# Products of pooled blocks in the middle of a projection unit instead of between two units

## Chip, cores and metric

The kernel runs on one core of a Trainium2 chip. The metric is the device time of one execution in microseconds, the median of several runs. A core has five engines with a queue of instructions each, which they work off in order: PE (TensorE, matrix products into PSUM), DVE (VectorE), ACT (ScalarE), POOL (GpSimd) and SP (SyncE, here only the issue of DMAs). They meet through semaphores: an instruction whose input is not there waits at the head of its queue, and what stands behind it waits too.

## What is computed

One layer of a hybrid encoder over 512 tokens of width 1024, all in float32. The part that matters here is the first sub-layer. The normalised input `h` is multiplied with one wide matrix `w_in`; its columns feed three mixers (a recurrence, a pooling mixer, a sparse attention) and three gates:

```python
h = rms_norm(x, g_mix_pre[l])
(lru_x, lru_gate, pool_in, q, k, v, q_idx, k_idx, w_idx,
 gate_logits) = split_columns(h @ w_in[l], IN_SIZES)
...
yb = multiscale_pool(pool_in, w_pool[l], pool_scale[l])
```

The pooling mixer takes trailing-window means over 2, 4, 8 and 16 tokens in four groups of 128 channels, subtracts the token itself, and multiplies each group with a 128x128 matrix:

```python
def multiscale_pool(p, w_pool, pool_scale):
    ...
    for g, w in enumerate(POOL_WINDOWS):
        start = jnp.maximum(t + 1 - w, 0)
        win_sum = cs[:, 1:, g] - cs[:, start, g]
        count = (t + 1 - start).astype(jnp.float32)[None, :, None]
        means.append(win_sum / count)
    pooled = jnp.stack(means, axis=2) - pf
    mixed = jnp.einsum('bsgc,gcd->bsgd', pooled, w_pool.astype(jnp.float32)).reshape(bsz, s, POOL_WIDTH)
    return (mixed * pool_scale.astype(jnp.float32)).astype(p.dtype)
```

After the mixers follow their merge, an output projection, cross-attention into 256 memory tokens and a SwiGLU feed-forward part.

## The kernel before

**Precision by halves.** Every float32 operand of a product is split into a rounded half (a cast on ACT) and the remainder (a subtraction on DVE or POOL). `mm3` (L89 to L92) issues three matmuls for one product: high by high, high by low, low by high. `halves` (L414 to L416) makes such a pair from a tile: L415 the cast on ACT, L416 the subtraction on DVE.

**Units.** The input stays on the chip, features on partitions, as the pair `hh`, `hl` (8 blocks of 128 features by 512 tokens). A *unit* is the projection of 128 columns of `w_in`: `unit_piece` (L406) runs `mm3` over the 8 feature blocks k = 0 to 7, so 24 matmuls of 128x512, into one PSUM tile. `unit` (L410) is a whole unit and then `give_w`, which gives the weight buffers free.

**Weights.** `take_w` hands out the next unit's weights and lets `prefetch` split ahead: a cast on ACT (L191) and a subtraction on DVE (L195) or in two halves on POOL (L198, L199). There are four buffers for each half, so a new split waits until an earlier unit has read its weights; its raw buffer is then loaded anew by a DMA on SP (L173).

**The stage of the change.** In this order there are four units for the recurrence, four for the pooling groups (`GROUPS` is 2, 0, 3, 1), and four for the queries of the attention. Work that belongs to a unit but needs its result later is kept in three queues of closures, `gates`, `pools` and `products`, and `settle(q, depth)` runs the oldest of a queue until only `depth` are left.

A pooled block goes through three steps. `pool_block(g, ps)` copies the unit's result out of PSUM on ACT (L628) and makes the window sums on POOL by doubling (L632, L633: one, two, three or four additions for windows of 2, 4, 8 or 16). Its `finish` divides and subtracts on DVE (L638, L640) and makes the halves `h`, `l` (L415 on ACT, L416 on DVE). The `product` it returns is one `mm3` on PE with the group's 128x128 matrix (three matmuls that read `h`, `l`, `h` in this order), then scales the result into `yb` (L648 on ACT, L649 on DVE). The products wait one turn each: the product of block 2 is issued in the turn of group 3, that of 0 in the turn of group 1, that of 3 with the first query unit, that of 1 with the second. The third and fourth query unit have none; nor have the first two pooling units.

In the same stretch DVE works off rounds of a top-k search for the attention (L495, L496), which `pump` takes from a background list a few at a time.

**What sets the order.** The program is written as one sequence, but a planner orders the queue of each engine when the kernel is compiled: it goes by the order in which things are written, moved forward or back by `tc.high_priority(offset=...)`, and by when it thinks their inputs are ready. Block work carries an offset that moves it forward (30 for `pool_block`, 100 for `finish`), the weight splits one that moves them back.

Of the kernel before, what the change touches and what calls it, by code (L numbers as in the profile page):

```python
# [17 lines left out]
S = 512  # L18
KD = D // P
# [46 lines left out]
def hybrid_block_kernel(ctx: ExitStack, tc: tile.TileContext, a: dict, out: bass.AP):  # L66
# [22 lines left out]
    def mm3(o, lh, ll, rh, rl, start, stop):  # L89
        T.matmul(o, lh, rh, start=start, stop=False, skip_group_check=True)  # L90
        T.matmul(o, lh, rl, start=False, stop=False, skip_group_check=True)  # L91
        T.matmul(o, ll, rh, start=False, stop=stop, skip_group_check=True)  # L92
# [6 lines left out]
    def pump(ns):  # L99
        while bg and ns > 0:  # L100
            cost, fn = bg.popleft()
            fn()
            ns -= cost
# [75 lines left out]
    def low_on(engines):  # L179
        low[:] = engines  # L180
# [32 lines left out]
    def take_w(ahead=None):  # L213
        while state["split"] <= state["taken"]:
            split_next()
        w = ready.popleft()
        state["taken"] += 1
        prefetch(ahead)
        return w

    def give_w(*ws):
        for w in ws:
            w[2]()
# [45 lines left out]
    ps = PS.take([P, 8])  # L269
# [4 lines left out]
    for q in range(2):  # L274
        ps = PS.take([P, 4, P])
# [130 lines left out]
    def unit_piece(o, w, c0, c1, ks=range(KD)):  # L406
        for k in ks:
            mm3(o[:, c0:c1], w[0][:, k], w[1][:, k], hh[:, k, c0:c1], hl[:, k, c0:c1], k == 0, k == KD - 1)

    def unit(o, w):  # L410
        unit_piece(o, w, 0, S)
        give_w(w)
# [18 lines left out]
    def stacked_queries(src, dst, m):  # L431

        h, l = T2.take([P, S], F32R), T2.take([P, S], F32R)
        halves(src, h, l)
        SP.dma_start(f32(dst[0][0:64, m]), f32(h[0:64]))
        SP.dma_start(f32(dst[0][64:128, m]), f32(l[0:64]))
        SP.dma_start(f32(dst[1][64:128, m]), f32(h[64:128]))
        SP.dma_start(f32(dst[1][0:64, m]), f32(l[64:128]))
        T2.give(h, l)
# [68 lines left out]
    for m in range(1, 4):  # L508
        w = take_w()
        ps = PS.take([P, S])  # L510
# [15 lines left out]
    w = take_w()  # L526
    ps = PS.take([P, S])
# [69 lines left out]
    def lru_roots():  # L597
        for m in range(4):
            sq.append(T2.take([P, S]))
            A.activation(sq[m], tP[:, m], AF.Sqrt)  # L600
# [24 lines left out]
    def pool_block(g, ps):  # L625
        w = 2 << g
        x_, s0, s1 = T2.take([P, S]), T2.take([P, S]), T2.take([P, S])
        A.copy(x_, ps)  # L628
        PS.give(ps)
        src, dst, other, d = x_, s0, s1, 1  # L630
        while d < w:
            G.tensor_add(dst[:, d:], src[:, d:], src[:, :S - d])  # L632
            G.tensor_copy(dst[:, :d], src[:, :d])  # L633
            src, dst, other, d = dst, other, dst, 2 * d

        def finish():
            with tc.high_priority(offset=100):
                V.scalar_tensor_tensor(src[:, :w - 1], src[:, :w - 1], float(w), inv[:, :w - 1],  # L638
                                       op0=OP.mult, op1=OP.mult)
                V.scalar_tensor_tensor(x_, src, 1.0 / w, x_, op0=OP.mult, op1=OP.subtract)  # L640
                h, l = T2.take([P, S], F32R), T2.take([P, S], F32R)
                halves(x_, h, l)
            T2.give(x_, s0, s1)

            def product():
                pz = PS.take([P, S])
                mm3(pz, wpl[:, 0, g], wpl[:, 1, g], h, l, True, True)
                A.activation(yb[0][:, g], pz, AF.Copy, scale=pscale(g))  # L648
                V.scalar_tensor_tensor(yb[1][:, g], pz, pscale(g), f32(yb[0][:, g]),  # L649
                                       op0=OP.mult, op1=OP.subtract)  # L650
                PS.give(pz)
                T2.give(h, l)
            return product
        return finish
# [7 lines left out]
    gates, pools, products = (collections.deque() for _ in range(3))  # L662

    def settle(q, depth, out=None):
        while len(q) > depth:
            r = q.popleft()()
            if out is not None:
                out.append(r)

    low_on("g")  # L670
    for m in range(4):
        w = take_w()
        ps = PS.take([P, S])
# [2 lines left out]
        gates.append(lru_block(m, ps))  # L676
        pump(800)
    low_on("v")
    for g in GROUPS:
        w = take_w()  # L680
        ps = PS.take([P, S])
        unit(ps, w)
        settle(gates, 1 if g == GROUPS[0] else 0)
        settle(products, 0)
        with tc.high_priority(offset=30):
            pools.append(pool_block(g, ps))
        settle(pools, 1, products)
        pump(1000)
    low_on("vg")
    Q = [K8.take([P, 4, S], F32R) for _ in range(2)]  # L690
    for m in range(4):
        w = take_w()
        ps = PS.take([P, S])
        unit(ps, w)
        settle(products, 0)
        stacked_queries(ps, Q, m)
        settle(pools, 0, products)
        PS.give(ps)
        if m == 1:
            lru_roots()  # L700
        pump(2300)
# [132 lines left out]
    for m in range(4):  # L834
        w = take_w()
        ps = PS.take([P, S])
# [159 lines left out]
    for m in range(4):  # L996
        w = take_w()
        ps = PS.take([P, NM])
# [19 lines left out]
    for i in range(4):  # L1018
        w = take_w()
# [67 lines left out]
    for h in range(4):  # L1087
        w = take_w()
        ps = PS.take([P, S])
# [335 lines left out]
```

## Time and profile before

| what | us |
|---|---|
| median of three runs (lowest, highest) | 884.73 (883.75, 884.84) |
| the profiled execution: its time | 883.94 |
| the profiled execution: span of the trace | 882.0 |
| PE busy in the span | 863.5 |
| DVE busy | 608.9 |
| ACT busy | 399.2 |
| POOL busy | 202.1 |
| the eight units of pooling and queries, with their products | 84.28 to about 136 on the span's clock |

In a row of the timeline stand the start on the span's clock, the duration, the engine, the line of the kernel, the operation and what it writes and reads; brackets give the engine's idle time ahead of it and what ended that. In the table by windows stand the stretch, its length, and for PE, weight loads, DVE, ACT and POOL the busy time with the number of instructions, then PE's granted clock, the share of the DMA engines and their rate. In a list of waits stand who waited, for whom, the sum, the times and the longest. `ps` is any PSUM tile, `hh` and `hl` the input, `wh` and `wl` weights of a unit, `t` any of ten work tiles of 128x512 (here mostly those of a block), `k` any of the larger tiles (here the pooling matrices and `yb`).

### The profile page before, as it was taken

The page shows a single profiled execution, that of the slowest core. Times are in us where ns is not written, and L with a number is a line of the kernel's source. Part 1 is how long each engine was busy: PE and PEld are TensorE (multiplying, and loading weights), DVE is VectorE, ACT ScalarE, POOL GpSimd, SP SyncE. Part 2 cuts the span into 40 slices and gives each one's busy share as a digit, 9 for nine tenths or more (in the row PEclk, how much of TensorE's full clock was granted, in tenths as well). Part 3 has the DMA queues.
Part 4 walks back from the last instruction along what each step waited for, and adds up shares of the span by engine and source line. Part 5 has one row for each costly group of instructions (what it writes and reads, how often), then busy time and mean ns, then how long its engine had stood idle before and what let it go on. Part 6 is the DMA issues. An engine that isn't in the chain of part 4 may idle for free.

```text
span 882.0 us, 12995 instructions
## 1 busy us (share of the span) xinstructions
PE 863.5 (98%) x4932; PEld 749.8 (85%) x4932; DVE 608.9 (69%) x1092; ACT 399.2 (45%) x669; POOL 202.1 (23%) x195
## 2 busy tenths in 40 slices
PE   7999999999999999999999999899999999999997
PEld 7888778888888888888888879899999999888885
DVE  7679989964864746342796788887888787732225
ACT  5455443323654445231565554545454555522121
POOL 2322455554434423210110010211111110000000
PEclk9999999999999999999999999999999999999999
DMA  8952237242332237333255301877677765333102
GB/s 246 251 128 76 79 96 192 71 119 80 89 96 72 60 108 260 99 96 95 91 186 154 96 1 36 168 167 174 150 155 157 174 161 143 120 96 96 48 1 97
DMA packets 128443, 105.52 MB, mean 120 GB/s; under 512 B 6200, under 2 KB 112252, under 8 KB 128380
## 3 DMA queue, kind: packets, MB, share of 16 engines
q1 hardware_dynamic: 120028, 89.99, 35.8%
q0 software_dynamic: 5760, 10.49, 7.6%
q10 hardware_dynamic: 2592, 4.20, 1.4%
q8 instruction: 39, 0.64, 0.3%
q14 instruction: 24, 0.20, 0.1%
HBM read 86.31 MB, written 2.10 MB: 100 GB/s over the span
## 4 chain that ended last, share of the span: by engine, by line
PE 81%; DVE 12%; POOL 2%; issue 2%; ACT 1%; DMA 1%; ACTq 0%; DVEq 0%; POOLq 0%
PE ps L91 25%; PE ps L92 25%; PE ps L90 25%; PE ps L473 2%; DVE k L938 1%; PE ps L800 1%; DVE k L954 1%; POOL t L632 1%; DVE hl L325 1%; DVE t L577 1%; DVE work L496 1%; DVE wl L195 1%; DVE m L495 1%; DVE k L963 1%; POOL y L296 1%
## 5 line engine op out<-in xcount | busy, mean ns | idle before, releaser
L191 ACT CAST wh<-raw 128x1024 fp32r<-128x1024 f32 (+1 forms) x104 | 108.5, 1045 | 226.8 <-PE ps L92 103.5
L90 PE MATMUL ps<-hh,wh 128*128 128x512 f32 (+2 forms) x584 | 207.1, 355 | 0.0
L91 PE MATMUL ps<-hl,wh 128*128 128x512 f32 (+2 forms) x584 | 206.2, 353 | 1.0 <-DVE hl L325 1.0
L92 PE MATMUL ps<-hh,wl 128*128 128x512 f32 (+2 forms) x584 | 206.4, 353 | 0.0
L195 DVE TENSOR_TENSOR wl<-raw,wh 128x1024 fp32r<-128x1024 f32 x60 | 74.5, 1246 | 102.8 <-ACT wh L191 102.8
L91 PEld LDWEIGHTS ps<-hl,wh 128*128 128x128 f32 (+1 forms) x584 | 109.1, 187 | 17.0 <-DVE hl L325 1.4
L90 PEld LDWEIGHTS ps<-hh,wh 128*128 128x128 f32 (+1 forms) x584 | 109.2, 187 | 15.9 <-ACT hh L324 0.2
L92 PEld LDWEIGHTS ps<-hh,wl 128*128 128x128 f32 (+1 forms) x584 | 109.0, 187 | 16.0
L90 PE MATMUL ps<-k,wh 128*128 128x256 f32 (+1 forms) x368 | 114.5, 311 | 0.0
L92 PE MATMUL ps<-k,wl 128*128 128x256 f32 (+1 forms) x368 | 113.8, 310 | 0.0
L91 PE MATMUL ps<-k,wh 128*128 128x256 f32 (+1 forms) x336 | 105.1, 313 | 0.0
L198 POOL TENSOR_TENSOR wl<-raw,wh 128x512 fp32r<-128x512 f32 (+1 forms) x44 | 59.3, 1348 | 148.4 <-ACT wh L191 134.2
L296 POOL TENSOR_TENSOR y<-u,half 128x1 f32<-128x1 f32 x26 | 16.0, 619 | 301.5 <-DVE u L293 260.7
L92 PE MATMUL ps<-wh,k 128*128 128x512 f32 x192 | 75.8, 395 | 0.0
L92 PEld LDWEIGHTS ps<-k,wl 128*128 128x128 f32 x368 | 69.2, 188 | 4.4
L90 PEld LDWEIGHTS ps<-k,wh 128*128 128x128 f32 x368 | 69.3, 188 | 4.2
L1215 DVE TENSOR_TENSOR wl<-raw,wh 128x1024 fp32r<-128x1024 f32 x40 | 48.9, 1225 | 31.7 <-ACT wh L1212 29.7
L91 PE MATMUL ps<-wl,k 128*128 128x512 f32 x176 | 69.4, 394 | 0.4 <-DVE wl L195 0.4
L1212 ACT CAST wh<-raw 128x1024 fp32r<-128x1024 f32 x40 | 42.0, 1049 | 61.2 <-PE ps L91 54.9
L90 PE MATMUL ps<-wh,k 128*128 128x512 f32 x176 | 69.0, 394 | 0.0
L91 PEld LDWEIGHTS ps<-k,wh 128*128 128x128 f32 x336 | 63.2, 188 | 4.2
L199 POOL TENSOR_TENSOR wl<-raw,wh 128x512 fp32r<-128x512 f32 (+1 forms) x44 | 61.3, 1393 | 0.0
(256 smaller groups left out, 1691.0 us busy)
## 6 DMA issues: line engine op xcount, KB each, us to landing
raw<-in_w_in SPq DMA_DIRECT2D x45, 512.0 KB, 4.3
raw<-in_w_ffn_in SPq DMA_DIRECT2D x44, 512.0 KB, 4.6
raw<-in_w_ffn_out SPq DMA_DIRECT2D x22, 512.0 KB, 3.6
raw<-in_w_branch SPq DMA_DIRECT2D x12, 512.0 KB, 3.5
raw<-raw POOLq DMA_DIRECT2D x20, 256.0 KB, 3.8
raw<-k POOLq DMA_DIRECT2D x20, 256.0 KB, 3.3
k<-t SPq DMA_DIRECT2D x32, 128.0 KB, 3.0
raw<-in_w_out SPq DMA_DIRECT2D x8, 512.0 KB, 3.5
```

Of the source, the lines that this page charges most:

```text
L90: T.matmul(o, lh, rh, start=start, stop=False, skip_group_check=True)
L91: T.matmul(o, lh, rl, start=False, stop=False, skip_group_check=True)
L92: T.matmul(o, ll, rh, start=False, stop=stop, skip_group_check=True)
L191: copy = A.copy(h, src)
L195: V.tensor_sub(l, src, f32(h))
L198: G.tensor_sub(l[:, :c], src[:, :c], f32(h[:, :c]))
L199: G.tensor_sub(l[:, c:], src[:, c:], f32(h[:, c:]))
L296: G.tensor_tensor(y, u, half, op=OP.pow)
L325: queued(V.tensor_sub(hl[:, 4 * q:4 * q + 4, dst], ps, f32(h)))
L473: T.matmul(ps[:, :n], q[j][:, hp, r], k[i][:, :n], start=i == 0, stop=i == 1, skip_group_check=True)
L1212: copy = A.copy(h, src)
L1215: V.tensor_sub(l, src, f32(h))
```

## The change

A new function `unit_around` takes the place of `unit` in the four pooling units and the four query units. It issues the first half of the unit (k = 0 to 3, 12 matmuls), then whatever waits in `products`, then the second half, and then gives the weights free. The `settle(products, 0)` behind the unit goes. So a product that was written behind the 24th matmul of its unit is now written behind the 12th; the unit's own end is written behind the product. In the pooling loop the products now also come ahead of `settle(gates, ...)`, though no turn has both.

```diff
     low_on("v")
+    def unit_around(ps, w):
+
+        unit_piece(ps, w, 0, S, range(4))
+        settle(products, 0)
+        unit_piece(ps, w, 0, S, range(4, KD))
+        give_w(w)
+
     for g in GROUPS:
         w = take_w()
         ps = PS.take([P, S])
-        unit(ps, w)
+        unit_around(ps, w)
         settle(gates, 1 if g == GROUPS[0] else 0)
-        settle(products, 0)
         with tc.high_priority(offset=30):
             pools.append(pool_block(g, ps))
         settle(pools, 1, products)
...
     for m in range(4):
         w = take_w()
         ps = PS.take([P, S])
-        unit(ps, w)
-        settle(products, 0)
+        unit_around(ps, w)
         stacked_queries(ps, Q, m)
         settle(pools, 0, products)
         PS.give(ps)
```

## The prediction

> **What bounds the kernel now.** I read the page first: span, engine totals, granted clock.
>
> ```profile
> span 882.0 us, 12995 instructions
> PE 863.5 (98%) x4932; PEld 749.8 (85%) x4932; DVE 608.9 (69%) x1092; ACT 399.2 (45%) x669; POOL 202.1 (23%) x195
> PEclk9999999999999999999999999999999999999999
> ```
>
> PE is busy for 863.5 of 882.0 us at full clock. So a change of order can win only what PE waits for, and costs only what new waits it makes PE suffer. Next I cut the stage of the change into units and products (table by windows; first number after the stretch is its length, then PE busy).
>
> ```profile
> 103.75:105.19 1.44, 0.96 (x4) 0.49 (x3) 1.44 (x4) 0.00 (x0) 0.00 (x0) 1.00 0.48 110
> 105.19:110.69 5.50, 5.50 (x25) 4.51 (x24) 5.50 (x12) 2.65 (x4) 3.21 (x4) 1.00 0.23 68
> 110.69:111.39 0.70, 0.70 (x5) 0.56 (x3) 0.70 (x3) 0.00 (x0) 0.62 (x2) 1.00 0.00 0
> 111.39:116.98 5.59, 5.59 (x26) 4.51 (x24) 4.45 (x14) 2.09 (x4) 2.50 (x5) 1.00 0.36 94
> 123.27:125.25 1.98, 1.24 (x5) 0.67 (x4) 1.98 (x6) 1.98 (x4) 0.00 (x0) 1.00 0.00 0
> ```
>
> I name the units that have a product beside them by their columns: U3 (pooled group 3, ends 103.75), U1 (ends 110.69), Q0 (first query unit, ends 116.98), Q1 (ends 123.27). Behind them come the products p2, p0, p3, p1 of the pooled blocks 2, 0, 3, 1, three matmuls each. A unit is 24 matmuls in 5.59 us, 0.233 us each, so half a unit is 2.79 us. A product whose inputs are there takes 0.70 us (p0). p2 takes 1.44 and p1 1.98: PE loses 0.74 + 1.28 = 2.02 us here. That is all there is to win.
>
> What does a product wait for? Its first and third matmul read h (the rounded half of the pooled block, ACT, L415), its second reads l (the remainder, DVE, L416). PE, then DVE, on the timeline:
>
> ```profile
> 98.25 0.40 PE L90 MATMUL ps<-hh,wh 128*128 128x512 f32 x1
> ...
> 101.02 0.39 PE L90 MATMUL ps<-hh,wh 128*128 128x512 f32 x1
> ...
> 103.75 0.40 PE L90 MATMUL ps<-t,k 128*128 128x512 f32 x1
> 104.63 0.50 PE L91 MATMUL ps<-t,k 128*128 128x512 f32 x1 [0.48 <-DVE t L416]
> ...
> 105.19 0.40 PE L90 MATMUL ps<-hh,wh 128*128 128x512 f32 x1
> ...
> 124.68 0.50 PE L91 MATMUL ps<-t,k 128*128 128x512 f32 x1 [0.56 <-DVE t L416]
> ```
> ```profile
> 103.90 0.67 DVE L416 TENSOR_TENSOR t<-t,t 128x512 fp32r<-128x512 f32 x1
> ...
> 106.04 0.68 DVE L416 TENSOR_TENSOR t<-t,t 128x512 fp32r<-128x512 f32 x1
> ...
> 113.56 0.17 DVE L638 SCALAR_TENSOR_TENSOR t<-t,inv 128x15 f32<-128x15 f32 x1 [1.14 <-POOL t L633]
> ...
> 115.64 0.68 DVE L416 TENSOR_TENSOR t<-t,t 128x512 fp32r<-128x512 f32 x1
> ...
> 121.48 0.16 DVE L638 SCALAR_TENSOR_TENSOR t<-t,inv 128x3 f32<-128x3 f32 x1 [2.05 <-POOL t L633]
> ...
> 123.95 0.68 DVE L416 TENSOR_TENSOR t<-t,t 128x512 fp32r<-128x512 f32 x1
> ```
>
> The four L416 end at 104.57, 106.72, 116.32 and 124.63. U3 starts at 98.25 and is at its middle at 101.02 (its 13th matmul); U1, Q0 and Q1 reach theirs at 107.98, 114.18 and 120.48 (starts 105.19, 111.39, 117.68 plus 2.79). So in the middle of its unit only p0 has its l. p2's comes 3.5 us later, p3's 2.1, p1's 4.1.
>
> What sets those times is a chain beside PE. ACT and POOL in this stage:
>
> ```profile
> 98.30 0.70 ACT L586 ACTIVATE t<-ps,ph 128x512 f32<-128x512 f32 x1
> 101.08 0.62 ACT L415 CAST t<-t 128x512 fp32r<-128x512 f32 x1 [2.08 <-DVE t L640]
> 101.60 0.68 ACT L587 ACTIVATE t<-ps,ph 128x512 f32<-128x512 f32 x1
> ...
> 105.27 0.62 ACT L415 CAST t<-t 128x512 fp32r<-128x512 f32 x1 [2.28 <-DVE t L640]
> 105.79 1.04 ACT L191 CAST wh<-raw 128x1024 fp32r<-128x1024 f32 x1
> 106.74 0.58 ACT L628 COPY t<-ps 128x512 f32<-128x512 f32 x1
> ...
> 114.89 0.62 ACT L415 CAST t<-t 128x512 fp32r<-128x512 f32 x1 [6.98 <-DVE t L640]
> 115.41 1.04 ACT L191 CAST wh<-raw 128x1024 fp32r<-128x1024 f32 x1
> 116.36 0.58 ACT L628 COPY t<-ps 128x512 f32<-128x512 f32 x1
> ...
> 122.95 0.62 ACT L415 CAST t<-t 128x512 fp32r<-128x512 f32 x1 [5.42 <-DVE t L640]
> 123.48 1.04 ACT L191 CAST wh<-raw 128x1024 fp32r<-128x1024 f32 x1
> 124.42 0.68 ACT L648 ACTIVATE k<-ps,pc 128x512 fp32r<-128x512 f32 x1
> ```
> ```profile
> 107.40 1.04 POOL L632 TENSOR_TENSOR t<-t 128x511 f32<-128x511 f32 x1 [7.37 <-ACT t L628]
> ```
>
> L628 copies a finished unit out of PSUM, POOL makes the window sums, DVE (L638, L640) the mean, ACT h, DVE l. Block 3's copy at 106.74 starts POOL; DVE waits 1.14 us for its sums; ACT stands 6.98 us before h of block 3; only then come the weight cast (L191) and block 1's copy, at 116.36, though U1 was over at 110.69. Thus block 1's chain starts where block 3's ends, and l of p1 at 124.63 is the end of one chain that begins at 106.74.
>
> **The change part by part.** Nothing is added or taken away: the same 24 + 3 matmuls per unit, the same tile slots in the same order, no DMA moved. Only a product's place goes from behind its unit to behind the unit's 12th matmul; its drain (L648 on ACT, L649 on DVE) may go earlier with it, and the unit's end, with what waits for it, comes 0.70 us or more later.
>
> Does PE's queue really take the product in the middle? The queues are ordered at compile time by a planner that passes over what it thinks not ready, as this late stretch shows, where one unit matmul slips in before the last of eight L800:
>
> ```profile
> 319.33 1.94 PE L800 MATMUL ps<-k,vv 128*128 128x512 f32 x7
> 321.12 0.39 PE L90 MATMUL ps<-hh,wh 128*128 128x512 f32 x1
> 321.35 0.40 PE L800 MATMUL ps<-k,vv 128*128 128x512 f32 x1
> ```
>
> So the question is when the planner thought h and l ready, and the ACT queue tells. h of block 1 (122.95) and a weight cast stand ahead of p3's drain L648 (124.42), which can go as soon as p3 is done, 0.70 us behind Q0 (117.68). A planner that prefers ready work would not have put them first unless it held h of block 1 ready by then, some 5 us earlier than it came; p1's middle of Q1 is 2.8 us after that. Likewise h of block 3 stands ahead of the copy of U1, that is, it was planned by about 110.7 and came at 115.51. And h of block 2 (101.08) stands between the two tanh (L586, L587) of a gate whose matmuls end where U3 starts, at 98.25: planned done by about 99.6, with l some 1.3 us behind (one DVE operation and L416), so by about 101, which is U3's middle. All three products therefore go to the middle, or within a few matmuls of it, and PE then waits there in earnest, since a matmul behind a waiting one in the queue does not pass it.
>
> The sum, on the clock of this execution. p2: l at 104.57, second half of U3 from 105.19 as p2's follower now, so U3 ends at 105.19 + 2.79 = 107.98 instead of 103.75. The weight cast ahead of block 3's copy takes the buffers of U3's own weights, so it moves from 105.79 to about 108.0, and the copy, 0.95 behind, to 108.95: 2.2 us later than 106.74, and with it the whole chain: l of p3 at 118.5, l of p1 at 126.8. PE meanwhile: U1 with p0 inside (no wait) from 107.98 to 114.27; Q0 reaches its middle at 117.06, waits for p3's l until 118.5, goes on at 119.1, ends at 121.9; Q1 reaches its middle at 124.7, waits until 126.8, goes on at 127.45 and ends at 130.24. Now the next unit starts at 125.25. That is **+5.0 us**.
>
> The unknown is how far the chain moves. Put shortly, PE leaves Q1 at l of p1 + 0.62 + 2.79 instead of l of p1 + 0.62: +2.8 us if the chain does not move at all, +5.0 if it moves by 2.2. If the copy is put ahead of the weight cast it moves by about 1.3 (108.0 against 106.74), and the sum is +4.1. I take the middle of the last two, +4.5: the cast stands ahead of the copy in both of the quoted places, but some reordering of ACT and DVE is sure. A reordering that puts L649 in front of block work on DVE would make that work wait for L648; I estimate that at 1 us (the 0.70 of an activation of this size, L586, and some queueing), so the upper end is +6.
>
> Does anything later give it back? From 126 to 420 us PE has one wait, and is busy throughout:
>
> ```profile
> 126.00:205.00 79.00, 79.00 (x344) 64.20 (x343) 65.79 (x113) 26.94 (x33) 44.81 (x33) 1.00 0.48 127
> ```
> ```profile
> PE ps L800 <- DVE k L416: 0.2, 1, 0.2
> ```
>
> So at most 0.2 us there; the later waits hang on PE's own results and move along. The new waits are covered by nothing, since a unit's second half stands behind the product.
>
> Longer waits could also lower the clock. The longest wait that I can check is 2.5 us late in the kernel, after which the clock is full:
>
> ```profile
> PE ps L90 <- ACT t L1274: 2.5, 1, 2.5
> ```
> ```profile
> 560.00:562.00 2.00, 1.90 (x16) 1.90 (x17) 2.00 (x3) 1.62 (x3) 0.00 (x0) 1.00 0.99 248
> ```
>
> My longest wait without a matmul is 2.9 us (h of p2 lets its first matmul go at 101.74; the second goes at 104.63). [...]
>
> **The rivals.** *The place does not move in the queue* (17%): the planner holds l ready only near the unit's end, so the products stay about where they are: within 1 us of 884.7. For it: all four stand right behind their unit now, and nothing in the PE rows shows a product earlier than that. Against it: the order they were written in forbade it until now, and the ACT queue above speaks for an early plan.
>
> *The waits are filled* (8%, the faster side): if the planner sees l late, it has 12 matmuls of the same unit to put ahead of each product's second matmul, where now it stalls. It decides from the point where the planned l is no earlier than the real one, 104.57 for p2 and 124.63 for p1. It gains both stalls, 2.02 us: 882.7. Against it: the planner is early by about 5 us for blocks 1 and 3.
>
> *The clock falls at p2* (4%): a wait somewhat longer than mine, and 12 matmuls at half speed cost 2.8 us more: about 892.
>
> **How the numbers follow.** The forecast has 71%: 883.94 (this execution's time, 1.94 around its span) + 4.5 = 888.4; the median of the three runs is 884.73, 0.79 above, so I set 884.73 + 4.5 = 889.2. The forecast's own range is +2.8 to +6: 887.5 to 890.7. To hold 8 in 10 the range takes in part of the first rival: 884.5 to 890.8. About 0.2% (1.8 us) is what a measurement of this kernel can tell from no change: faster 0.08, same 0.17, slower 0.75 (forecast and fallen clock).
>
> **What would show it.** Right: the three t,k matmuls of each product stand between the 12th and 13th matmul of U3, U1, Q0 and Q1; PE waits there for L416 about 3.4 us at p2, none at p0, 1.4 at p3 and 2.0 at p1 (6.8 against 2.0); block 3's copy L628 starts near 109; the query unit behind p1 starts near 130. Wrong: products that still stand at the unit's end, or l of p1 earlier than 124, which would mean that ACT or DVE was reordered in the chain's favour; or PE waits after 126 us that shrink.

## The result and the profile after

| | before | after |
|---|---|---|
| median (lowest to highest) | 884.24 (883.09 to 884.84), 4 runs | 893.51 (893.34 to 893.55), 4 runs |
| ratio, 95% interval | | 1.0103 (1.009 to 1.0115) |
| the profiled execution: time, span | 883.94, 882.0 | 893.34, 891.4 |
| its mean granted clock (1 is full clock) | 0.999 | 0.992 |

The change costs 9.27 us. The forecast was +4.5: the sign was right, the size half of what came, and 893.51 lies above the range.

First the page of after: its span and its engine totals (busy us, share of the span, instructions).

```profile
span 891.4 us, 12991 instructions
PE 869.1 (97%) x4932; PEld 753.7 (85%) x4932; DVE 607.4 (68%) x1092; ACT 399.9 (45%) x669; POOL 201.9 (23%) x195
```

PE still issues 4932 matmuls, but it is busy 5.6 us longer than before (863.5). So this is not only waiting: the same matmuls take longer. The other 3.8 us of the longer span (9.4) are idle time.

The waits of PE in the whole kernel of after (who waited, for whom, the sum, how often, the longest):

```profile
PE ps L91 <- DVE t L416: 4.3, 3, 2.4
...
PE ps L90 <- ACT t L415: 2.2, 2, 1.6
PE ps L90 <- ACT t L1279: 2.1, 1, 2.1
```

The first two are the products' waits for l and h, 6.5 us together where the forecast had 6.8; the third stands far behind the stage, ahead of the feed-forward part. Next the table by windows of after (stretch, length, then busy time and instructions of PE, weight loads, DVE, ACT and POOL, then the granted clock, the DMA share, GB/s). The first row is the whole stage, the others single pieces of it, the last a piece far behind it.

```profile
98.00:140.00 42.00, 35.46 (x135) 27.06 (x134) 35.53 (x84) 16.98 (x25) 19.21 (x23) 0.92 0.34 88
104.00:106.00 2.00, 2.00 (x8) 1.63 (x9) 2.00 (x5) 1.21 (x2) 0.00 (x0) 0.84 0.82 236
106.00:108.00 2.00, 2.00 (x6) 1.52 (x6) 2.00 (x7) 0.00 (x0) 0.00 (x0) 0.50 0.02 4
130.00:132.00 2.00, 2.00 (x6) 1.52 (x5) 2.00 (x4) 1.58 (x3) 0.84 (x1) 0.50 0.68 159
570.00:573.00 3.00, 3.00 (x16) 3.00 (x16) 2.75 (x5) 0.67 (x2) 0.58 (x1) 0.50 1.21 302
```

In the stage PE got 135 matmuls done in 42 us. Twice in it the granted clock stands at 0.50, with 6 matmuls listed in 2 us, where 0.233 us each would make eight or nine. The timeline shows where that begins and ends (start, duration, engine, line, operation, brackets with the idle time ahead and its releaser):

```profile
97.45 0.40 PE L90 MATMUL ps<-hh,wh 128*128 128x512 f32 x1
...
103.83 0.51 PE L91 MATMUL ps<-t,k 128*128 128x512 f32 x1 [2.38 <-DVE t L416]
...
104.40 0.40 PE L90 MATMUL ps<-hh,wh 128*128 128x512 f32 x1
...
105.33 0.59 PE L91 MATMUL ps<-hl,wh 128*128 128x512 f32 x1
105.72 0.63 PE L92 MATMUL ps<-hh,wl 128*128 128x512 f32 x1
...
108.28 0.62 PE L92 MATMUL ps<-hh,wl 128*128 128x512 f32 x1
108.71 0.43 PE L90 MATMUL ps<-hh,wh 128*128 128x512 f32 x1
...
119.08 0.50 PE L91 MATMUL ps<-t,k 128*128 128x512 f32 x1 [0.64 <-DVE t L416]
...
127.06 0.49 PE L90 MATMUL ps<-t,k 128*128 128x512 f32 x1 [1.65 <-ACT t L415]
...
128.80 0.50 PE L91 MATMUL ps<-t,k 128*128 128x512 f32 x1 [1.24 <-DVE t L416]
...
129.45 0.63 PE L90 MATMUL ps<-hh,wh 128*128 128x512 f32 x1
...
133.70 0.40 PE L90 MATMUL ps<-hh,wh 128*128 128x512 f32 x1
```

U3 starts at 97.45, 0.80 earlier than before (a wait for the first DMA at the head of the kernel was 2.3 us instead of 3.1), so times are best taken from there. p2 stands in the middle of U3 and waits. Its second half starts at 104.40 and should take 2.79 us; it takes 4.31, to 108.71. The slow matmuls begin at 105.33, 1.5 us after PE had resumed; the starts at 108.28 and 108.71 are 0.43 us apart, where 0.233 is usual. The second half of Q1 (129.45 to 133.70) takes 4.25 instead of 2.79 in the same way. From U3's start to the start of Q2, the unit behind Q1, it is 133.70 - 97.45 = 36.25 us, where before it was 125.25 - 98.25 = 27.00: **+9.25 us**, which is the whole loss. The rest of the kernel cancels to 0.2 us in this pair of profiles (-0.80 at the head, -0.41 up to the feed-forward part, +1.37 from there on; there too is a stretch at half clock, the row at 570).

Last the chain beside PE, in after: ACT, POOL and DVE on the timeline.

```profile
108.52 1.05 ACT L191 CAST wh<-raw 128x1024 fp32r<-128x1024 f32 x1 [2.85 <-PE ps L91]
109.47 0.58 ACT L628 COPY t<-ps 128x512 f32<-128x512 f32 x1
...
118.74 0.58 ACT L628 COPY t<-ps 128x512 f32<-128x512 f32 x1
...
126.39 0.62 ACT L415 CAST t<-t 128x512 fp32r<-128x512 f32 x1 [5.13 <-DVE t L640]
```
```profile
123.80 1.29 POOL L608 TENSOR_TENSOR t<-t,k 128x512 f32<-128x512 f32 x1
```
```profile
123.88 1.23 DVE L638 SCALAR_TENSOR_TENSOR t<-t,inv 128x3 f32<-128x3 f32 x1 [2.47 <-POOL t L633]
...
125.63 0.67 DVE L640 SCALAR_TENSOR_TENSOR t<-t,t 128x512 f32<-128x512 f32 x1
...
126.89 0.87 DVE L495 MAX8 m<-work 128x8 f32<-128x256 f32 x2
...
128.07 0.68 DVE L416 TENSOR_TENSOR t<-t,t 128x512 fp32r<-128x512 f32 x1
```

POOL in before, for comparison:

```profile
127.60 3.81 POOL L608 TENSOR_TENSOR t<-t,k 128x512 f32<-128x512 f32 x3 [6.16 <-ACT t L600]
```

The cast of the weights ahead of block 3's copy came as worked out, but later, because U3 ended later. From U3's start the copy is at 12.02 instead of 8.49 (+3.53). l of p1 ends at 128.75, 31.30 behind U3's start, instead of 26.38 (+4.92). So 1.39 us more were lost between the two. They are lost behind block 1's copy: from that copy's start to the end of l it takes 128.75 - 118.74 = 10.01 us, before 124.63 - 116.36 = 8.27. That is 1.74 more, of which a shorter time between the two copies (9.27 us instead of 9.62) gives 0.35 back. The 1.74 have two parts. L638, which takes 0.16 us before, takes 1.23 and ends together with POOL's L608 (123.80 + 1.29 = 125.09; 123.88 + 1.23 = 125.11). And L416 starts 1.06 us after h is there (126.39 + 0.62 = 127.01) instead of 0.38 before (123.57 to 123.95), since DVE still does top-k work. L608 multiplies with the square roots of the recurrence (L600 on ACT). In after the first root is taken at 120.63, ahead of h of block 1; in before L608 runs only from 127.60 on, behind block 1.

### The profile page after: what moved, and what is told of

It is laid out like the page before. It is cut to its first block, busy times and chain, and to the rows that moved or that the text cites. A ratio compares the mean times of both kernels' runs of the same rounds, so it can differ in the third digit from the quotient of the medians.

```text
span 891.4 us, 12991 instructions
## 1 busy us (share of the span) xinstructions
PE 869.1 (97%) x4932; PEld 753.7 (85%) x4932; DVE 607.4 (68%) x1092; ACT 399.9 (45%) x669; POOL 201.9 (23%) x195
## 4 chain that ended last, share of the span: by engine, by line
PE 81%; DVE 12%; issue 3%; POOL 2%; ACT 1%; DMA 1%; DVEq 0%; ACTq 0%; POOLq 0%
PE ps L91 26%; PE ps L92 26%; PE ps L90 25%; PE ps L473 2%; DVE k L943 1%; PE ps L805 1%; DVE k L959 1%; DVE t L577 1%; DVE hl L325 1%; DVE work L496 1%; DVE wl L195 1%; DVE m L495 1%; DVE k L968 1%; POOL y L296 1%; PE ps L790 1%
## 5 line engine op out<-in xcount | busy, mean ns | idle before, releaser
L90 PE MATMUL ps<-hh,wh 128*128 128x512 f32 (+2 forms) x584 | 208.6, 357 | 0.0
L90 PEld LDWEIGHTS ps<-hh,wh 128*128 128x128 f32 (+1 forms) x584 | 110.2, 189 | 16.1 <-ACT wh L1217 0.2
L90 PE MATMUL ps<-k,wh 128*128 128x256 f32 (+1 forms) x368 | 114.4, 311 | 0.0
L198 POOL TENSOR_TENSOR wl<-raw,wh 128x512 fp32r<-128x512 f32 (+1 forms) x44 | 59.8, 1359 | 154.8 <-ACT wh L191 140.6
L90 PEld LDWEIGHTS ps<-k,wh 128*128 128x128 f32 x368 | 69.3, 188 | 4.2
L90 PE MATMUL ps<-wh,k 128*128 128x512 f32 x176 | 69.0, 394 | 0.0
```

What stands on the lines that cost most here:

```text
L198: G.tensor_sub(l[:, :c], src[:, :c], f32(h[:, :c]))
```

## The experiments

My theory after this: the products lose 8.20 us instead of 2.02, so +6.2, and the clock adds two stretches of about 1.5 us each. "Lost" is what a product's place takes on PE beyond the 0.70 us of its three matmuls: 104.40 - (97.45 + 2.79 + 0.70) = 3.46 at p2, 1.25 at p3 (119.08 is its second matmul, Q0 goes on at 119.66), and 3.49 at p1. The rivals: the excess is the chain alone, or a worse order of ACT and DVE; or the clock falls for a reason other than these waits. For each profile I take one measure, from U3's first matmul to the first matmul that reads `k` with weights `wh` (PE, L90), some 50 us later; before has 98.25 to 147.38, 49.13 us. "Falls" are stretches at granted clock 0.50 in it, "lost" is the sum over the products.

| kernel | median (lowest to highest), runs | ratio, 95% interval | stage | lost | falls |
|---|---|---|---|---|---|
| before | 884.24 (883.09 to 884.84), 4 | | 49.13 | 2.02 | 0 |
| after | 893.51 (893.34 to 893.55), 4 | 1.0103 (1.009 to 1.0115) | 58.37 | 8.20 | 2 |
| after, again | 894.5 (892.71 to 895.52), 4 | 1.0106 (1.0092 to 1.012) | 58.39 | 8.75 | 2 |
| middle in pooling units only | 889.29 (886.44 to 890.42), 6 | 1.0044 (1.0031 to 1.0057) | 52.29 | 3.59 | 1 |
| middle in query units only | 891.65 (891.22 to 892.0), 5 | 1.0073 (1.006 to 1.0086) | 55.71 | 5.58 | 2 |
| waits of p2 and p1 filled | 888.13 (887.94 to 888.35), 5 | 1.0034 (1.0022 to 1.0046) | 55.09 | 8.04 | 0 |
| wait of p2 alone filled | 888.45 (887.51 to 889.91), 6 | 1.0044 (1.0031 to 1.0057) | 55.15 | 8.05 | 0 |
| square roots two turns later | 890.88 (888.34 to 892.31), 6 | 1.0063 (1.0047 to 1.008) | 55.53 | 6.82 | 1 |
| weight cast behind the copy | 887.91 (887.57 to 889.22), 6 | 1.0038 (1.0026 to 1.005) | 52.06 | 4.96 | 0 |
| behind the 18th matmul | 885.73 (884.85 to 887.99), 12 | 1.0017 (1.0008 to 1.0026) | 51.13 | 4.08 | 0 |
| middle, one turn later | 881.43 (880.56 to 883.9), 5 | 0.9964 (0.9952 to 0.9976) | 47.05 | 0 | 0 |
| end of the unit, one turn later | 882.88 (881.59 to 884.02), 7 | 0.9978 (0.9968 to 0.9989) | 47.04 | 0 | 0 |

Ratios are against runs of before on the same chip in the same batch (medians 884.24, then 885.04, 884.75 and 885.1).

The stage adds up. In the six kernels without a fall it differs from before's by lost - 2.02 to within 0.07 us (the product behind the 18th matmul: 51.13 - 49.13 = 2.00, and 4.08 - 2.02 = 2.06). In the five with falls there remain 1.3 to 1.6 us for each (the query units alone: 6.58 - 3.56 = 3.0 for two).

### The change in the pooling units alone

Only the pooling loop calls `unit_around`; the query loop is that of before.

```diff
     for m in range(4):
...
-        unit_around(ps, w)
+        unit(ps, w)
+        settle(products, 0)
```

> The changed kernel with the middle place only in the four pooling units; p3 and p1 stand behind their query units again. My theory (waits at the early products, and half clock after the long ones): the wait at p2 stays (3.5 us) and the granted clock falls behind it as in the changed kernel (12 matmuls take 4.3 us instead of 2.8); U3 ends some 5.7 us late, block 3's copy and with it l of p1 come about 3.7 us late, p3 has no wait, PE leaves p1 3.7 us later than before: about +3.7 us (888.0). Rival 1 (the clock does not matter, only the waits): the chain moves by 2.2, +2.2 us (886.5). Rival 2 (only the two products in query units matter): within 1 us of before.

The median came 4.25 us above before, and the stage 3.16 us. The profile shows p2's loss again (3.47 us) and one stretch at half clock behind it, none later in the stage (there is one more at 528 us). A window of this kernel:

```profile
106.00:108.00 2.00, 2.00 (x7) 1.52 (x6) 2.00 (x8) 0.00 (x0) 0.00 (x0) 0.50 0.02 4
```

p3 and p1, at the ends of their units, lose nothing and 0.12 us: 3.59 - 2.02 = 1.57, and 1.59 remain for the fall. This half agrees with the theory. The run times spread by 4 us, and the profiled execution (886.44) is the fastest of the six; the other experiments with falls take the spread up again.

### The change in the query units alone

```diff
     for g in GROUPS:
...
-        unit_around(ps, w)
+        unit(ps, w)
         settle(gates, 1 if g == GROUPS[0] else 0)
+        settle(products, 0)
```

> The changed kernel with the middle place only in the four query units; p2 and p0 stand behind their units again. My theory: l of p3 and p1 come at the times of before (116.3 and 124.6 on its clock), PE waits about 2.0 us at each and leaves Q1 half a unit later than now: +2.8 us (887.0); the waits are shorter than at p2 of the changed kernel, so the clock may stay (if it falls once, +1.5 more: 888.6). Rival (the harm is done at p2 alone): within 1 us of before.

A miss: 6.61 us above before, though U3 and U1 stand as before. PE on the timeline, two windows, and POOL and DVE, all of this kernel:

```profile
115.24 0.50 PE L90 MATMUL ps<-t,k 128*128 128x512 f32 x1 [1.25 <-ACT t L415]
...
116.06 0.50 PE L91 MATMUL ps<-t,k 128*128 128x512 f32 x1 [0.32 <-DVE t L416]
```
```profile
118.00:120.00 2.00, 2.00 (x6) 1.58 (x5) 1.11 (x2) 1.14 (x2) 1.92 (x4) 0.50 0.06 8
128.00:130.00 2.00, 2.00 (x6) 1.54 (x5) 2.00 (x3) 1.44 (x3) 1.10 (x2) 0.50 0.64 148
```
```profile
121.09 1.29 POOL L608 TENSOR_TENSOR t<-t,k 128x512 f32<-128x512 f32 x1
```
```profile
121.16 1.23 DVE L638 SCALAR_TENSOR_TENSOR t<-t,inv 128x3 f32<-128x3 f32 x1 [2.05 <-POOL t L633]
```

Two things that I had not allowed for. The clock fell behind p3 after waits of only 1.25 and 0.32 us, and again behind p1. And l of p1 was 2.25 us later than before though U3 and U1 had not moved: L608 stands beside L638, as in after, which makes 1.07 us of it; the other 1.18 are DVE's top-k work between h and L416 (1.56 us instead of 0.38). So the second delay belongs to the change itself and not to U3's lateness: the planner brings the square roots forward and puts more top-k work ahead of l when the products leave the ends of the query units.

### The waits filled with matmuls that nobody reads

All as after, but `product()` of blocks 2 and 1 issues extra matmuls into a spare PSUM tile: 3 ahead of p2 and 9 between its first and second matmul, 7 and 5 for p1. It adds 24 matmuls that the result doesn't use.

```diff
+                fill = {2: (3, 9), 1: (7, 5)}.get(g, (0, 0))
+                spare = PS.take([P, S]) if any(fill) else None
                 pz = PS.take([P, S])
-                mm3(pz, wpl[:, 0, g], wpl[:, 1, g], h, l, True, True)
+                for _ in range(fill[0]):
+                    T.matmul(spare, wpl[:, 0, g], hh[:, 0], start=True, stop=True)
+                T.matmul(pz, wpl[:, 0, g], h, start=True, stop=False, skip_group_check=True)
+                for _ in range(fill[1]):
+                    T.matmul(spare, wpl[:, 0, g], hh[:, 0], start=True, stop=True)
+                T.matmul(pz, wpl[:, 0, g], l, start=False, stop=False, skip_group_check=True)
+                T.matmul(pz, wpl[:, 1, g], h, start=False, stop=True, skip_group_check=True)
+                if any(fill):
+                    PS.give(spare)
```

> The changed kernel with extra matmuls, whose result nobody reads, put into the waits of two products: 3 ahead of p2's first matmul and 9 behind it, 7 and 5 at p1, sized below the waits that the changed kernel shows there. My theory (half clock after the waits costs 3.0 us of the 9.3): the granted clock stays full from 98 to 140 us, the second halves of U3 and Q1 take 2.8 us each again, and the time is about 890.3, 3 us below the changed kernel. Rival (the time lost is that of the waits, and the clock rows only show them in another way): no change against the changed kernel, 893.5, or slower by what the extra matmuls take.

The stage as one window:

```profile
98.00:140.00 42.00, 40.76 (x173) 31.91 (x172) 39.66 (x96) 18.36 (x27) 22.69 (x26) 1.00 0.27 71
```

With 24 matmuls more the kernel is 5.4 us faster than after (888.13 against 893.51). The clock is 1.00 throughout, and the stage is 3.28 us shorter than after's. Its loss against before, 55.09 - 49.13 = 5.96, is what the products alone explain (8.04 - 2.02 = 6.02). So in the stage the two falls cost about 3 us, and PE's idle time in it is what brings them: the five executions have a mean clock of 0.998 or 0.999, the eight of after (both times) 0.991 to 0.995. The remaining 2 us came outside the stage: the wait ahead of the feed-forward part is 0.8 us here, and no fall follows it.

### The wait of p2 alone filled

As above with `fill = {2: (3, 9)}`.

> The changed kernel with the extra matmuls at p2 alone (3 ahead of its first matmul, 9 behind it), none at p1. My theory: the fall behind p2 goes, U3 ends 1.5 us earlier, and block 3's copy and the whole chain with it; PE and chain both gain 1.5, so p1's wait stays about 3.4 us and its fall stays: about 1.5 us below the changed kernel in the stage, 891.5 to 892.3. Rival (one fall brings the other about): both go, as with both waits filled, 888 to 889.

The time came to 888.45, below what I expected. p1 in the middle of Q1 (its first and second matmul are L651 and L654 of this kernel), and the stretch behind it:

```profile
125.76 0.50 PE L651 MATMUL ps<-t,k 128*128 128x512 f32 x1 [1.65 <-ACT t L415]
...
127.50 0.50 PE L654 MATMUL ps<-t,k 128*128 128x512 f32 x1 [1.24 <-DVE t L416]
```
```profile
128.00:130.00 2.00, 2.00 (x10) 1.59 (x10) 2.00 (x5) 2.00 (x4) 1.31 (x1) 1.00 0.60 139
```

The same two waits as in after, with the same matmuls behind them, and here the clock stays at 1.00. So with p2 alone filled both falls are gone in this execution, and the length of a wait does not settle whether a fall follows. That the filling of p2 spared p1 is not shown; the last section shows what differs at p1.

### The square roots two turns later

```diff
-        if m == 1:
+        if m == 3:
             lru_roots()
```

> The changed kernel with the square roots of the recurrence written two query units later, so that their ACT and POOL work (L600, L608) does not come among block 1's. My theory of the extra lateness of p1's l: a POOL multiplication (L608, 1.29 us) beside the small DVE operation L638 stretches that from 0.16 to 1.23 us, and more top-k work slips in ahead of L416; without it l of p1 comes 1 to 2 us earlier and so does the time: 891.4 to 892.5. Rival (that lateness is all from the late end of U3): no change, 893.5.

DVE, and two windows (half clock lies in the first only):

```profile
124.85 0.16 DVE L638 SCALAR_TENSOR_TENSOR t<-t,inv 128x3 f32<-128x3 f32 x1 [2.46 <-POOL t L633]
```
```profile
98.00:128.00 30.00, 25.09 (x96) 18.63 (x94) 23.37 (x54) 12.06 (x19) 14.12 (x18) 0.94 0.25 71
128.00:140.00 12.00, 11.69 (x51) 9.63 (x52) 12.00 (x32) 6.08 (x9) 9.13 (x7) 1.00 0.56 136
```

The median, 890.88, is 0.5 us below the lower end of what I expected. With L608 away L638 takes 0.16 us again, and p1 loses 1.94 us instead of 3.49: that the roots make 1.55 us of it is shown. The fall behind p1 is gone too, another 1.5 us. The six runs fall into two groups, 888.34 and 888.38 at a mean clock of 0.999, and 890.8 to 892.31 at 0.992 to 0.995: one and the same kernel has the falls in some executions and not in others.

### The weight cast behind block 3's copy

The last three matmuls of a unit are reordered, so that the one that frees `wh` is not ahead of the one that ends the unit's PSUM tile.

```diff
-        unit_piece(ps, w, 0, S, range(4, KD))
+        unit_piece(ps, w, 0, S, range(4, KD - 1))
+        k = KD - 1
+        T.matmul(ps, w[0][:, k], hh[:, k], start=False, stop=False, skip_group_check=True)
+        T.matmul(ps, w[1][:, k], hh[:, k], start=False, stop=False, skip_group_check=True)
+        T.matmul(ps, w[0][:, k], hl[:, k], start=False, stop=True, skip_group_check=True)
```

> The changed kernel with the last three matmuls of each of these units in another order (high by high, low by high, high by low), so that the high weights are read by the unit's very last matmul; the ACT queue then has the copy of a finished unit ahead of the next weight cast, and block 1's cast ahead of the square roots. My theory (block 3's copy stands 0.95 us behind the weight cast, and block 1's again): l of p3 comes about 1 us earlier, l of p1 about 2 to 4 us, and the time falls by as much: 889.5 to 891.5. Rival (ACT's order does not set l): no change, 893.5.

ACT, where U3 ends, in this kernel:

```profile
108.00 0.59 ACT L628 COPY t<-ps 128x512 f32<-128x512 f32 x1 [2.13 <-PE ps L687]
...
108.48 1.05 ACT L191 CAST wh<-raw 128x1024 fp32r<-128x1024 f32 x1
```

The copy went ahead of the cast, at 9.76 us from U3's start (98.24) instead of 12.02, and l of p1 ended 26.53 behind that start instead of 31.30. The stage is 6.3 us shorter than after's, of which 3.2 are smaller losses and the rest the two falls. It is not a clean test of the cast: in this kernel the square roots come behind h of block 1, so L638 meets no L608, and p2, which loses 3.27 us, is followed by no fall. L638 meets a POOL subtraction of the weight split instead (L198, 1.29 us from 119.96 on) and takes 1.10 us. What the cast alone is worth stays open. The time, 887.91, lies 1.6 us below the lower end of what I expected.

### The product behind the 18th matmul

`range(4)` and `range(4, KD)` become `range(6)` and `range(6, KD)`.

> The changed kernel with the product behind the 18th matmul of its unit (k = 0 to 5, then 6 and 7) instead of the 12th. My theory (what is lost is the wait until l comes, plus what of the unit still stands behind it, plus the clock where half of a stretch of 3.4 us is idle): p2 waits about 2.0 us, block 3's copy comes 0.8 us later than before, p1 has half the rest of unit behind it (1.4 us), so +2.2 to +4.4 against before (887.2 to 889.4), about 5 us below the changed kernel; a fall of the clock would add 1.5. Rival (any place inside the unit costs the same, by the order alone): as the changed kernel, +9.

The products lose 2.12, 0.47 and 1.49 us, 4.08 instead of 8.20, and in the profiled execution the clock does not fall in the stage. (Its mean clock is 0.999; the two slowest of the twelve, 887.68 and 887.99 us, have 0.993 and 0.995.) The time is 1 us above before and 1.5 us below the lower end of what I expected.

### The product one turn later, in the middle of the next unit

```diff
-    def unit_around(ps, w):
+    def unit_around(ps, w, keep=1):
...
-        settle(products, 0)
+        settle(products, keep)
...
-        unit_around(ps, w)
+        unit_around(ps, w, 1 if m < 2 else 0)
```

The first `keep` is that of the pooling loop, the last line is in the query loop. Each product comes 24 matmuls later than in after.

> The changed kernel with each product kept one turn longer: p2 in the middle of U1, p0 of Q0, p3 of Q1, p1 of the third query unit. The middle place stays, but every l is there long before. My theory: no wait at any product, full clock; the 2.0 us that the kernel before loses at p2 and p1 go too: 882.2, about 2 us below before. Rival (the place inside a unit costs by itself, through the later end of each unit and of the weight buffers): slower than before by 1 us or more.

PE in the stage as a window, and the first matmul of p2 on the timeline:

```profile
98.00:140.00 42.00, 42.00 (x184) 34.24 (x183) 36.56 (x90) 19.81 (x31) 26.51 (x28) 1.00 0.40 107
```
```profile
106.80 0.39 PE L90 MATMUL ps<-t,k 128*128 128x512 f32 x1
```

p2 has no bracket: its h and l are there. PE is busy 42.00 of 42 us. The stage is 2.08 us shorter than before, which is the 2.02 us of stalls that before has. The time is 3.6 us below before's in the same batch, so 1.5 us of it are not in this stage. I can't place them: the two profiled executions differ by only 1.66 us (883.94 and 882.28), and this one has a fall of the clock at 524 us that before's has not.

### The product one turn later, at the end of a unit

Before with `settle(products, 1)` in the pooling loop and `settle(products, 1 if m < 2 else 0)` in the query loop; no unit is split.

> The kernel before with each product kept one turn longer, behind the whole unit (p2 behind U1, p0 behind Q0, p3 behind Q1, p1 behind the third query unit). My theory (only the wait for l counts, not the place): no wait at the products, as with the middle place one turn later: 881 to 882.5, within 1 us of that run. Rival (the middle place is better by itself once inputs are there): 1 us or more above that run.

The stage is 47.04 us, equal to the 47.05 of the kernel above. The median is 0.4 us above the range that I expected and 1.45 us above that of the kernel above, as the rival would have it. But the two come from two batches, the intervals of the ratios overlap, and the stage does not hold the difference. So the gain comes from the turn, not from the middle.

### After, once more

> The changed kernel once more, as a measure for the run with the extra matmuls at p2 alone, on the same chip. My theory: at p2 and p1 the wait fills nearly all of a stretch of 3.4 us, so the clock falls behind both in every run: 893 to 894, with little spread, and two stretches of half clock between 98 and 140 us. Rival (the falls come by chance, as in the run without the early roots, whose times spread over 4 us with their clock): a spread of 3 us or more.

The ratio to before (1.0106, the first time 1.0103) and the two falls in the stage came again (58.39 us against 58.37, waits and falls at the same places). The spread did not: 2.8 us where the first four runs agree within 0.21. Outside the stage its profile has two further falls, at 535 and 570 us; the first profile of after has the one at 570 too.

## Why the prediction was wrong

**What bounds the kernel: right.** Behind the stage after gets 0.41 us back at the wait ahead of the feed-forward part and nothing else, and in the stage the two kernels with the products one turn later gained the 2.02 us that were called all there is to win.

**The place in the queue: right.** All four products stand between the 12th and the 13th matmul. The planner takes h and l as ready early, and PE waits for them in earnest.

**The loss at p2: right** (3.46 us, forecast 3.45), **at p0: right** (none), **at p3: nearly** (1.25, forecast 1.4), **at p1: not** (3.49, forecast 2.0).

**l of p1 at 126.8: failed.** "PE leaves Q1 at l of p1 + 0.62 + 2.79" has the right form, but its first term was mis-sized. On the clock of before it is 124.63 + 4.92 = 129.55 instead of 126.8. Two terms were missing:
- U3's end was taken 2.79 behind the restart, but eight of the second half's twelve matmuls ran at half clock, so block 3's copy moved by 3.53 and not by 2.2: +1.3.
- The chain between copy and l was moved as it stood. The planner moved the square roots into it, L638 took 1.23 us beside L608 instead of 0.16 (+1.07), and DVE did more top-k work ahead of l (+0.68), of which 0.35 came back between the two copies: +1.4. "Some reordering of ACT and DVE is sure" was there, but as a range of 1 us about L649; POOL, which held the real one, was read for block 3's sums only. The kernel with the roots two turns later shows this term (1.55 us of p1's loss go).

**The clock: failed.** The sum had full clock throughout. The fallen clock was a rival at 4%, at p2 alone, for a wait longer than mine, and at 2.8 us. No run shows that the wait has to be longer than mine, and none shows the 2.8 us: the clock fell at p2 and p1, at waits as long as mine, and that costs 1.52 and 1.46 us, since it lasts 3.41 us and not for all twelve matmuls. The second is a direct term, since Q1's second half stands behind p1: +1.5. My row for "no fall after 2.5 us" was a true row and no proof: in after that same place has a wait of 2.1 us and a fall. The falls lie on a grid of stretches of 3.413 us (last section), and the prediction asked for the length of a wait alone.

The sum with these terms: 5.0 + 1.3 + 1.4 + 1.5 = 9.2, measured 9.25 in the stage. The shading from +5.0 to +4.5, for a copy ahead of the cast, was in the wrong direction.

**The range** took the forecast's own bounds for the chain and gave the clock almost nothing, so its upper end (890.8) fell short by 2.7 us.

## What to carry to other kernels

A consumer that was written earlier than its input is ready did not overlap with anything on PE's queue here: it stopped the ready work behind it (3.46 us lost at p2, with twelve matmuls of U3 behind it), and the same work written a turn later gained what the stall cost (47.05 us for the stage instead of 49.13, and 58.37 for the middle). When such waits leave PE about half idle for some 3 us (0.84 to 1.84 us of work in 3.41 ahead of the falls in this stage), price the clock as well, at about 1.5 us each time (1.52 and 1.46 in after), as a case with a real chance and not as a remote one (where the wait lies in the grid of the last section bears on it, and that differs from one execution to the next), and once more for every chain that hangs on the delayed work. When a place in the program's order moves, look at every engine for what the planner will put into the gap, POOL too.

## What the runs showed of the hardware

**In these traces the clock falls for one stretch of a grid of 3.413 us, after a stretch that PE spends about half idle.** In after the first fall lasts from 105.36 to 108.77 (eight matmuls at 0.43 us instead of 0.233) and begins with PE at work again, 1.5 us behind the wait there; the second lasts from 129.25 to 132.66. Their ends are 23.9 us apart, which is 7 times 3.413. In the kernel with the query units alone the two end at 120.53 and 130.77, 10.24 apart, which is 3 times it. The traces keep each change of the granted clock with its time. In after that record starts at 6.37 us of the span, and the three falls ahead of the last matmul last 3.413 us each and begin 29, 36 and 165 times 3.413 us behind its start. The windows of the other kernels with several falls agree to within 0.1 us: after once more has falls at about 105.42, 129.30, 535.50 and 569.64 (7, 126 and 136 times 3.413 us behind the first), the kernel with the roots later at about 105.66, 532.32 and 566.46 (125 and 135 times). Where the stretches lie differs from one execution to the next: the record starts at 6.56 us in before and at 6.37 in after. The two stretches at p2 and the two at p1 in after, and two at p1 with p2 alone filled, are these (stretch, length, PE busy; the clock is third from the end of a row). With p2 filled the stage has no fall to count from, so that grid is an estimate, counted as in after from the start of the record (6.53 us).

```profile
101.95:105.36 3.41, 1.53 (x7) 1.26 (x8) 3.41 (x9) 1.13 (x3) 0.00 (x0) 1.00 0.55 140
105.36:108.77 3.41, 3.41 (x10) 2.64 (x9) 3.41 (x9) 0.56 (x2) 0.00 (x0) 0.50 0.06 16
125.84:129.25 3.41, 0.95 (x3) 0.60 (x4) 3.41 (x9) 2.10 (x4) 0.00 (x0) 1.00 0.03 7
129.25:132.66 3.41, 3.41 (x10) 2.62 (x9) 3.41 (x7) 2.38 (x4) 1.83 (x2) 0.50 0.66 151
```
```profile
122.58:125.99 3.41, 1.76 (x8) 1.09 (x6) 3.35 (x8) 0.90 (x2) 1.27 (x2) 1.00 0.19 66
125.99:129.41 3.42, 2.19 (x9) 1.60 (x9) 3.42 (x10) 2.66 (x5) 1.16 (x1) 1.00 0.33 77
```

In after both waits of p1, but for the first 0.4 us, lie in one stretch, which leaves 0.95 us of work in it, and the next stretch has half clock. With p2 filled a border of the estimated grid at 125.99 cuts the same waits into stretches with 1.76 and 2.19 us of work, and the clock stays. In the stage the eight stretches ahead of a fall have 0.84 to 1.84 us of work (1.53 and 0.95 in after, 1.02 and 0.84 in after once more, 1.03 with the pooling units alone, 1.84 and 1.25 with the query units alone, 1.02 with the roots later), and no stretch without a fall behind it has less than the 1.76. Later in the kernel a fall follows 1.44 us in after (from 566.16 on) and 2.04 us in the kernel with the product in the middle one turn later (the 3.4 us ahead of 523.8), and none follows the 1.51 us in before (from 556.11 on, at the wait of 2.5 us). So the falls of these runs go by these stretches, and no exact limit is shown. None of these stretches was idle as a whole: in the kernel with the query units alone the clock fell after waits of 1.25 and 0.32 us, 0.5 us apart, and in the 3.4 us ahead of that fall PE was busy for 1.84 us (in after, ahead of 105.36, for 1.53). Why no fall follows 1.51 us and one follows 2.04, and why after's first four runs agree so well, is open.

**L638, a tiny DVE operation, ends together with the large POOL one beside it.** L638, on 3 columns, takes 0.16 us in before and 1.23 in after, beside POOL's 1.29 us multiplication L608 of two 128x512 tiles. L608 began 0.08 us earlier, and both end together (125.11 and 125.09). In the kernel with the query units alone L608 began 0.07 us ahead of L638, L638 took 1.23 us, and they end at 122.38 and 122.39. So it is with another POOL operation in the kernel with the weight cast behind the copy: L198 began 0.20 us ahead of L638 there, L638 took 1.10 us, and they end at 121.25 and 121.26. With the roots two turns later POOL had no work beside it, and it took 0.16 us. What holds L638 is not shown.
